# Row norm moved to ScalarE, weight and bias applied on transposed banks: one change to a Trainium2 block kernel

## The chip, the core and the metric

The kernel runs on one core of a Trainium2 chip. The metric is the device time of one execution in microseconds. The engines of the core are TensorE (PE, matmuls and transposes; PEld its weight loads), VectorE (DVE), ScalarE (ACT), GpSimd (POOL) and SyncE (SP, which here only issues DMAs). Each engine runs its own instructions strictly in the order in which they stand in its program, and waits on semaphores for the others.

## The reference, cut to what matters

The input is 1024 rows (two halves H = 0 and 1 of 512 rows, four row blocks of 128 in each) of width 1024. Attention and a depthwise convolution run side by side on a projection of x; their outputs, joined and projected, are added to the scaled residual. The part that the change touches:

```
r  = ALPHA * x + (concat(attention, conv) @ w_out + b_out)
x1 = layer_norm(r) * ln1_g + ln1_b            # over the 1024 columns of a row
u  = x1 @ w_up ; depthwise filter over rows ; silu(gate) * up ; f = (...) @ w_down
r2 = ALPHA * x1 + f                           # then the second layer norm
```

x1 is needed twice: transposed, as the left operand of the up-projection, and in rows, times ALPHA, as the residual of the second norm.

## The kernel before

The work is staged in halves. First come the input projections, convolution and attention of both halves; then `out_proj(0)` and `out_proj(1)` (four column quarters, in each the four row blocks), then the first norm `ln1` of each half, and `up` and `down` of each half. The stages overlap: while `out_proj(0)` runs, attention and the convolution taps of half 1 go on; while `ln1(0)` runs, attention's tail and the convolution's own norm (`conv_norm(1)`, L443 to L472) go on; and `ln1(1)` runs under the up-projection of half 0. A scheduler puts every engine's instructions in an order when the kernel is built, from readiness in its own timeline; nothing is reordered on the chip. So whoever adds an instruction changes the order of its neighbours too.

All matmuls are made in two pieces: a value is rounded to a "high" tensor by a ScalarE cast (`wh`, `oh`, `x`), and the rest, the "low" tensor (`wl`, `ol`), is the difference, taken on GpSimd for weights (L233) and on VectorE for activations (L282). A weight's `wl` therefore stands in GpSimd's queue, and whatever GpSimd does ahead of it delays the matmuls L268 that use it.

What the change touches:

- `out_proj`, L623: the four residual rows of a half are loaded into `acc` and VectorE makes `acc = ALPHA*x + b_out` (128x1024). The products of the two branches are added to `acc` quarter by quarter (L648, L650).
- `ln1`: `row_stats` (L298, L300, and the inverse root on GpSimd, L293), then `layer_norm_rows`: for both halves (LNM 0) VectorE subtracts and scales (L311), GpSimd multiplies by the weight `g1` (L312), VectorE adds the bias (L313). Then `transpose_split`: eight TensorE transposes into two PSUM banks (L278), ScalarE's cast (L281), VectorE's difference (L282). Last ScalarE multiplies the rows by ALPHA (L662).
- Attention's tail on the same engines: softmax sums on VectorE (L510 to L523), the scaling of the probabilities `hank` on GpSimd (L526), their transposes on TensorE (L537), the splits `ph` (L539 ScalarE, L540 VectorE), and the products L558 to L560.
- `up_branch`: products L265, L266 (high weights), L268 (low weights); then the row filter on VectorE (L676, L678) in `z`.
- For half 1 each block's banks are also summed by `other_sums` on VectorE (L747).

Of the kernel before, what the change touches and what calls it, by code (L numbers as in the profile page):

```python
# [15 lines left out]
P = 128  # L16
# [23 lines left out]
KOFF = (4, 5)  # L40
AHEAD = 1
LNM = (0, 0, 1, 1)
XM = (1, 1)
PT = {'x0': 'AT', 'x1': 'AS', 'glu0': 'AS', 'glu1': 'A', 'kv0': 'A', 'kv1': 'A', 'q0': 'A', 'q1': 'A', 'v0': 'T', 'v1': 'T',
      'joint': 'ATSACSYN',
      'tail': 'T', 'out0': 'A', 'out1': 'A', 'ln0': 'A', 'ln1': 'TCN', 'sum1': 'T', 'up0': 'A', 'up1': 'AY', 'down0': 'SY', 'down1': 'S'}
# [23 lines left out]
def hybrid_layer_kernel(  # L70
# [129 lines left out]
    nc.scalar.dma_start(out=pr1[34:78, :], in_=r128(ffn_dw_b))  # L200
    nc.scalar.dma_start(out=pr1[78:122, :], in_=r128(ffn_dw_w[2]))
    nc.scalar.dma_start(out=pr3[0:88, :], in_=ffn_dw_w[0:2].rearrange("k (r c) -> (k r) c", c=P))
    def parameters():
        tp = psB()
        for i, pr in enumerate((pr1, pr2, pr3)):
            nc.tensor.transpose(out=tp[:, i * P:(i + 1) * P], in_=pr, identity=ident)
        nc.vector.tensor_copy(out=par, in_=tp[:, 0:3 * P].rearrange("p (i c) -> p i c", c=P))
        nc.vector.tensor_scalar(out=bq8, in0=par[:, 0, 0:4], scalar1=-0.125, scalar2=None, op0=ALU.mult)

    def pcol(t, i):  # L210
# [9 lines left out]
    fdb = [pcol(0, 34 + i) for i in range(2 * NC)]  # L220
    fw = [[pcol(2, i) for i in range(2 * NC)], [pcol(2, 44 + i) for i in range(2 * NC)],
          [pcol(0, 78 + i) for i in range(2 * NC)]]

    def cdw(k, c):
        return pcol(1, k * 4 + c)
# [45 lines left out]
    def transpose_split(src, xh, xl, t, key):  # L271
        banks = []
        for q in range(2):
            b = psk(key)
            banks.append(b)
            for k in range(4):
                kt = q * 4 + k
                nc.tensor.transpose(out=b[:, k * P:(k + 1) * P], in_=src[:, kt * P:(kt + 1) * P], identity=ident)  # L278
            bv_ = b.rearrange("p (k t) -> p k t", t=P)
            hd = xh[q][:, :, t * P:(t + 1) * P]  # L280
            nc.scalar.copy(out=hd, in_=bv_)  # L281
            nc.vector.tensor_tensor(out=xl[q][:, :, t * P:(t + 1) * P], in0=bv_, in1=f(hd), op=ALU.subtract)  # L282
        return banks
# [370 lines left out]
    def ln1(H, g, b):  # L654
# [2 lines left out]
        x1T[H] = (xh, xl)  # L657
        for t in range(TB):
            a = acc[H * TB + t]
            layer_norm_rows(a, g, b, H)  # L660
            banks = transpose_split(a, xh, xl, t, "ln%d" % H)
            nc.scalar.mul(out=a, in_=a, mul=ALPHA)  # L662
            if H == 1:
                other_sums(t, *[b.rearrange("p (k t) -> p k t", t=P) for b in banks])
            yield
# [316 lines left out]

    def first_norm():
        norm1.extend((bcast_row(ln1_g, 'g1'), bcast_row(ln1_b, 'b1')))
        yield from ln1(0, *norm1)

    def second_conv_norm():
# [86 lines left out]
```

## Time and profile before

| what | value |
| --- | --- |
| median of 3 runs | 1112.66 us (1112.2 to 1114.48) |
| profiled execution | 1113.39 us |
| its span in the trace | 1111.6 us |
| TensorE busy | 1050.4 us, 94% |
| VectorE busy | 788.9 us, 71% |
| ScalarE busy | 481.9 us, 43% |
| GpSimd busy | 654.5 us, 59% |

The profiled execution is 0.7 us above the median, and 1.8 us of it lie outside the span. A matmul's duration is that of a pipelined instruction: rows of one line start closer together than they last. In a timeline a row is start, duration, engine, line, operation, output and inputs, how many, and in brackets the idle time of that engine just before it with what ended it. Durations with x2 or x4 are those of the whole row.

### The profile page before, as it was taken

To read this page: it belongs to the slowest core of one execution; us is meant where nothing else is said; L and a number is where in the kernel's file an instruction comes from. 1 tells how busy PE (TensorE), PEld (TensorE's weight loads), DVE (VectorE), ACT (ScalarE), POOL (GpSimd) and SP (SyncE) were. 2 spreads that over 40 slices of the span, in tenths; PEclk is the share of its full clock that TensorE was granted. 3 is DMA by queue.
4 is the path that set the end of the run, shared out by engine and by line. 5 is a ranking of instruction groups with operands and counts; after the bars stand their busy time and mean duration, and the time that the engine had idled before them with its cause. 6 is when DMAs were issued, how large, how long until landed. Compare 5 with 4: busy or idle time off the path is not lost.

```text
span 1111.6 us, 14383 instructions
## 1 busy us (share of the span) xinstructions
PE 1050.4 (94%) x5113; PEld 873.9 (79%) x5113; DVE 788.9 (71%) x1430; ACT 481.9 (43%) x915; POOL 654.5 (59%) x560
## 2 busy tenths in 40 slices
PE   7999999878968999898999999999999999999996
PEld 5887778778957998676788787878788787888875
DVE  2899789999897448985746656564747566569656
ACT  4546677753548333462515242433425142442430
POOL 3749688775587556455736372746556363636551
PEclk9999999999978999899999999999999999999999
DMA  6535221413600242131211021111212110233321
GB/s 183 160 87 132 77 57 40 139 53 98 186 20 1 78 132 65 50 110 43 76 37 59 20 82 32 58 56 38 76 39 76 35 60 20 76 114 115 113 95 75
DMA packets 115641, 85.19 MB, mean 77 GB/s; under 512 B 20354, under 2 KB 108017, under 8 KB 115569
## 3 DMA queue, kind: packets, MB, share of 16 engines
q1 hardware_dynamic: 112368, 78.92, 23.9%
q10 hardware_dynamic: 3201, 5.35, 1.4%
q8 instruction: 40, 0.66, 0.2%
q14 instruction: 32, 0.26, 0.1%
HBM read 80.05 MB, written 4.21 MB: 76 GB/s over the span
## 4 chain that ended last, share of the span: by engine, by line
PE 76%; DVE 13%; DMA 4%; POOL 3%; ACT 3%; issue 1%; SPq 0%; POOLq 0%; DVEq 0%; ACTq 0%
PE psA L265 6%; PE psA L266 6%; PE psA L268 5%; PE psS L713 2%; PE psS L714 2%; PE psS L715 2%; PE psS L796 2%; PE psS L794 2%; PE psS L793 2%; PE psA L794 2%; PE psA L796 2%; PE psA L793 2%; PE psS L505 2%; PE psA L638 1%; PE psA L713 1%
## 5 line engine op out<-in xcount | busy, mean ns | idle before, releaser
L233 POOL TENSOR_TENSOR wl<-raw,wh 128x512 fp32r<-128x512 f32 x196 | 263.3, 1355 | 162.2 <-ACT wh L231 68.9
L231 ACT CAST wh<-raw 128x512 fp32r<-128x512 f32 x196 | 119.1, 620 | 173.5 <-PE psA L266 24.1
L233 POOL TENSOR_TENSOR wl<-ts,wh 128x512 fp32r<-128x512 f32 x64 | 82.5, 1296 | 155.4 <-ACT wh L231 135.5
L421 DVE SCALAR_TENSOR_TENSOR psC<-hconv,const,psC 128x512 f32<-128x512 f32 x196 | 147.3, 751 | 3.5
L265 PE MATMUL psA<-x,wh 128*128 128x512 f32 x336 | 135.9, 404 | 7.9 <-DVE z L678 4.1
L266 PE MATMUL psA<-x,wh 128*128 128x512 f32 x336 | 134.4, 400 | 0.0
L231 ACT CAST wh<-ts 128x512 fp32r<-128x512 f32 x64 | 39.3, 622 | 177.4 <-PE psS L715 39.2
L268 PE MATMUL psA<-x,wl 128*128 128x512 f32 x336 | 87.2, 396 | 0.6 <-POOL wl L233 0.6
L265 PEld LDWEIGHTS psA<-x,wh 128*128 128x128 f32 x336 | 64.9, 193 | 23.9 <-issue 4.7
L266 PEld LDWEIGHTS psA<-x,wh 128*128 128x128 f32 x336 | 64.9, 193 | 13.5 <-issue 0.2
L268 PEld LDWEIGHTS psA<-x,wl 128*128 128x128 f32 x336 | 62.3, 188 | 15.1 <-issue 1.2
L293 POOL TENSOR_TENSOR tiny<-tiny,const 128x1 f32<-128x1 f32 (+1 forms) x28 | 26.5, 951 | 53.7 <-DVE tiny L292 50.7
L720 DVE TENSOR_TENSOR acc<-psS,acc 128x512 f32<-128x512 f32 x52 | 35.7, 688 | 31.4 <-PE psS L715 31.4
L233 POOL TENSOR_TENSOR ol<-or,oh 128x512 fp32r<-128x512 f32 x32 | 40.7, 1296 | 18.9 <-ACT oh L231 16.6
L793 PE MATMUL psA<-x,wh 128*128 128x512 f32 x112 | 43.6, 389 | 0.0
L794 PE MATMUL psA<-x,wh 128*128 128x512 f32 x112 | 43.6, 389 | 0.0
L793 PE MATMUL psS<-x,wh 128*128 128x512 f32 x112 | 43.6, 389 | 0.0
L794 PE MATMUL psS<-x,wh 128*128 128x512 f32 x112 | 43.6, 389 | 0.0
L832 POOL TENSOR_TENSOR ts<-raw,ts 128x512 f32<-128x512 f32 x32 | 42.0, 1313 | 1.3
L413 POOL TENSOR_TENSOR cp<-cp,cp 128x512 f32<-128x512 f32 x28 | 36.0, 1287 | 8.4 <-ACT cp L409 8.4
L713 PE MATMUL psS<-wh,gh 128*128 128x512 f32 x88 | 35.0, 397 | 5.9 <-ACT gh L693 3.1
L638 PE MATMUL psA<-oh,x 128*128 128x256 f32 x128 | 37.9, 296 | 1.9 <-ACT z L399 1.5
(383 smaller groups left out, 3057.9 us busy)
## 6 DMA issues: line engine op xcount, KB each, us to landing
raw<-in_w_up SPq DMA_DIRECT2D x56, 512.0 KB
raw<-in_w_down SPq DMA_DIRECT2D x28, 512.0 KB
raw<-in_w_in SPq DMA_DIRECT2D x20, 512.0 KB
raw<-in_x SPq DMA_DIRECT2D x8, 512.0 KB
raw<-in_w_in SPq DMA_DIRECT2D x16, 256.0 KB
acc<-in_x SPq DMA_DIRECT2D x8, 512.0 KB
or<-in_w_out SPq DMA_DIRECT2D x64, 64.0 KB
or<-in_w_out SPq DMA_DIRECT2D x8, 512.0 KB
```

The source lines that it names most:

```text
L231: nc.scalar.copy(out=h, in_=part)
L233: nc.gpsimd.tensor_tensor(out=l, in0=part, in1=f(h), op=ALU.subtract)
L265: m.append(nc.tensor.matmul(out=o, lhsT=wh[kt], rhs=xh[kt], start=kt == 0, stop=False))
L266: m.append(nc.tensor.matmul(out=o, lhsT=wh[kt], rhs=xl[kt], start=False, stop=False))
L268: m.append(nc.tensor.matmul(out=o, lhsT=wl[kt], rhs=xh[kt], start=False, stop=kt == KT - 1))
L421: tap(nc.vector.scalar_tensor_tensor(out=dst if k == KO else total, in0=src, scalar=cdw(k, c), in1=total, op0=ALU.mult, op1=ALU.add))
L638: m.append(nc.tensor.matmul(out=pa[:, 0, :], lhsT=yah[:, c, :], rhs=wa[0][c], start=c == 0, stop=False))
L713: m.append(nc.tensor.matmul(out=o, lhsT=gh[:, tsl], rhs=wh, start=j == 0, stop=False))
L793: m.append(nc.tensor.matmul(out=o, lhsT=wh[k], rhs=xh[k], start=k == 0, stop=False))
L794: m.append(nc.tensor.matmul(out=o, lhsT=wh[k], rhs=xl[k], start=False, stop=False))
L796: m.append(nc.tensor.matmul(out=o, lhsT=wl[k], rhs=xh[k], start=False, stop=k == 3))
L832: nc.gpsimd.tensor_tensor(out=t, in0=x0, in1=x1, op=ALU.subtract)
```

## The change

`out_proj` (both halves): ScalarE multiplies the loaded rows by ALPHA, and GpSimd adds the output bias; L623 on VectorE is gone. `ln1` (both halves): VectorE makes only a column, minus mean times inverse deviation (`shift`); ScalarE makes the plain normalised rows with it (one 128x1024 activation in place of L311). The transposes take these rows, and ScalarE multiplies and shifts each 128x128 piece of a transposed bank in place by that piece's weight and bias columns, four per bank, 64 in all, ahead of its cast. The rows that the second residual needs are made behind the transposes, by GpSimd alone: times `g1`, plus `b1`, both of which are scaled by ALPHA once by ScalarE. So L312 of before stays, moved behind the transposes; L313 (VectorE) becomes a GpSimd addition; L662 is gone. Weight and bias also come in as columns, by two more DMAs at the start.

```diff
-XM = (1, 1)
+XM = (0, 0)
...
+    nc.scalar.dma_start(out=pr3[88:96, :], in_=r128(ln1_g))
+    nc.scalar.dma_start(out=pr3[96:104, :], in_=r128(ln1_b))
...
+    l1g = [pcol(2, 88 + i) for i in range(KT)]
+    l1b = [pcol(2, 96 + i) for i in range(KT)]
...
+    def transpose_norm(src, xh, xl, t, key):
+        banks = []
+        for q in range(2):
+            b = psk(key)
+            banks.append(b)
+            for k in range(4):
+                kt = q * 4 + k
+                nc.tensor.transpose(out=b[:, k * P:(k + 1) * P], in_=src[:, kt * P:(kt + 1) * P], identity=ident)
+            for k in range(4):
+                kt = q * 4 + k
+                col = b[:, k * P:(k + 1) * P]
+                nc.scalar.activation(out=col, in_=col, func=AF.Identity, bias=l1b[kt], scale=l1g[kt])
             bv_ = b.rearrange("p (k t) -> p k t", t=P)
             hd = xh[q][:, :, t * P:(t + 1) * P]
             nc.scalar.copy(out=hd, in_=bv_)
...
-            layer_norm_rows(a, g, b, H)
-            banks = transpose_split(a, xh, xl, t, "ln%d" % H)
-            nc.scalar.mul(out=a, in_=a, mul=ALPHA)
+            mv, rstd = row_stats(a)
+            shift = ring("shift1", 1, 2)
+            nc.vector.scalar_tensor_tensor(out=shift, in0=mv[:, 0:1], scalar=-1.0, in1=rstd, op0=ALU.mult, op1=ALU.mult)
+            nc.scalar.activation(out=a, in_=a, func=AF.Identity, bias=shift, scale=rstd)
+            banks = transpose_norm(a, xh, xl, t, "ln%d" % H)
+            nc.gpsimd.tensor_tensor(out=a, in0=a, in1=g, op=ALU.mult)
+            nc.gpsimd.tensor_tensor(out=a, in0=a, in1=b, op=ALU.add)
...
         norm1.extend((bcast_row(ln1_g, 'g1'), bcast_row(ln1_b, 'b1')))
+        for row in norm1:
+            nc.scalar.mul(out=row, in_=row, mul=ALPHA)
```

In the changed kernel the lines stand lower; the new ones are L301 (the activation on a bank), L648 and L649 (residual rows on ScalarE and GpSimd), L685 (`shift`), L686 (rows on ScalarE), L688 and L689 (rows on GpSimd). L549 is the old L526, L424 the old L401, L446 the old L423, L316 the old L293, L238 the old L233, L304 the old L281, L236 the old L231, L297 the old L278, L270 the old L265.

GpSimd at the start of `out_proj(0)`; `vpad` and `x_10` belong to attention, `hank` are its probabilities, `ol` a low weight of `out_proj`. Before:

```order
L381 MEMSET vpad_76_1909 128x512
L293 TENSOR_TENSOR tiny_0_60<-tiny_0_60,const_1_61 128x4
L526 TENSOR_SCALAR hank_34_254<-hank_34_254,tiny_0_60 128x256 x2
L526 TENSOR_SCALAR hank_35_256<-hank_35_256,tiny_0_60 128x256 x2
L401 TENSOR_TENSOR x_10_91<-z_43_342,x_9_90 128x512
L233 TENSOR_TENSOR ol_87_2135<-or_85_2124,oh_86_2133 128x512
```

The same place in the changed kernel:

```order
L649 TENSOR_TENSOR acc_81_2114<-acc_81_2114,bo_80_2112 128x1024
L649 TENSOR_TENSOR acc_82_2118<-acc_82_2118,bo_80_2112 128x1024
L424 TENSOR_TENSOR x_10_93<-z_45_409,x_9_92 128x512
L649 TENSOR_TENSOR acc_83_2122<-acc_83_2122,bo_80_2112 128x1024
L404 MEMSET vpad_76_1911 128x512
L649 TENSOR_TENSOR acc_84_2126<-acc_84_2126,bo_80_2112 128x1024
L316 TENSOR_TENSOR tiny_0_60<-tiny_0_60,const_1_61 128x4
L446 TENSOR_TENSOR cy_73_1511<-cy_73_1511,cp_61_946 128x512
L549 TENSOR_SCALAR hank_34_256<-hank_34_256,tiny_0_60 128x256 x2
L549 TENSOR_SCALAR hank_35_258<-hank_35_258,tiny_0_60 128x256 x2
```

The four bias additions now stand ahead of the probabilities' scaling and of the first low weights.

ScalarE at the end of `ln1(0)`, around the last block's second bank (`psA_3178` before, `psA_3213` after, cast into the part of x1 named `x_38`); `cy`, `x_11` and `nsq` belong to `conv_norm(1)`, `wh` is an up-projection weight. Before:

```order
L281 CAST x_38_262<-psA_3178 128x4x128
L662 ACTIVATE acc_84_2121<-acc_84_2121 128x1024
L539 CAST ph_63_1090<-psT_3227 128x512
L467 ACT_TABLE_LOAD
L467 ACTIVATE cy_72_1508<-cy_72_1508,const_1_61 128x512
```

And in the changed kernel, from that bank's first activation:

```order
L301 ACTIVATE psA_3213<-psA_3213,const_1_61 128x128
L491 ACTIVATE x_11_94<-cy_73_1511,const_1_61 128x512
L495 ACTIVATE nsq_102_2945<-cy_73_1511 128x512
L490 ACTIVATE cy_75_1513<-cy_75_1513,const_1_61 128x512
L236 CAST oh_126_3660<-or_116_3517 128x512
L491 ACTIVATE x_11_94<-cy_74_1512,const_1_61 128x512
L495 ACTIVATE nsq_103_2948<-cy_74_1512 128x512
L301 ACTIVATE psA_3213<-psA_3213,const_1_61 128x128
L491 ACTIVATE x_11_94<-cy_75_1513,const_1_61 128x512
L495 ACTIVATE nsq_104_2951<-cy_75_1513 128x512
L236 CAST wh_25_205<-raw_44_348 128x512
L301 ACTIVATE psA_3213<-psA_3213,const_1_61 128x128 x2
```

Where the cast of the last bank stood ahead of the convolution norm's activations (L467, L468, L472; now L490, L491, L495), it now follows nearly all of them: the bank's cast is the next row. Two units of attention's products, which stood among the matmuls of the first up-projection, now stand ahead of it on TensorE.

GpSimd during `ln1(1)`; `wl_23` is a low weight of the up-projection that runs at the same time. Before:

```order
L312 TENSOR_TENSOR acc_114_3467<-acc_114_3467,g1_105_2972 128x1024
L312 TENSOR_TENSOR acc_115_3470<-acc_115_3470,g1_105_2972 128x1024
L233 TENSOR_TENSOR wl_137_3878<-raw_128_3860,wh_131_3866 128x512
L233 TENSOR_TENSOR wl_146_4384<-raw_133_3870,wh_134_3872 128x512
L233 TENSOR_TENSOR wl_130_3864<-raw_133_3870,wh_136_3876 128x512
L233 TENSOR_TENSOR wl_21_170<-raw_44_346,wh_25_203 128x512
L233 TENSOR_TENSOR wl_23_174<-raw_44_346,wh_27_207 128x512
```

The same place in the changed kernel:

```order
L238 TENSOR_TENSOR wl_21_172<-raw_44_348,wh_25_205 128x512
L688 TENSOR_TENSOR acc_113_3505<-acc_113_3505,g1_105_2978 128x1024
L689 TENSOR_TENSOR acc_113_3505<-acc_113_3505,bo_80_2112 128x1024
L688 TENSOR_TENSOR acc_114_3509<-acc_114_3509,g1_105_2978 128x1024
L238 TENSOR_TENSOR wl_23_176<-raw_44_348,wh_27_209 128x512
L689 TENSOR_TENSOR acc_114_3509<-acc_114_3509,bo_80_2112 128x1024
```

Three row operations stand between two low weights of one product that followed each other before (`b1` shares the buffer named `bo`).

## Rows read from the trace of the kernel before

**Rows 1.** The page's first part: busy time, share and instructions of each engine.
```profile
PE 1050.4 (94%) x5113; PEld 873.9 (79%) x5113; DVE 788.9 (71%) x1430; ACT 481.9 (43%) x915; POOL 654.5 (59%) x560
```

**Rows 2.** Stretches: from:to, length, busy time by engine, granted clock, DMA share, GB/s.
```profile
core 0: us, PE busy (x) PEld busy (x) DVE busy (x) ACT busy (x) POOL busy (x), PEclk, DMA share, GB/s
200.00:300.00 100.00, 88.33 (x635) 80.45 (x634) 93.18 (x215) 52.76 (x141) 66.44 (x77) 0.98 0.35 110
300.00:346.00 46.00, 33.71 (x178) 27.84 (x178) 43.46 (x93) 24.08 (x59) 34.89 (x33) 0.74 0.13 45
346.00:425.00 79.00, 79.00 (x534) 73.12 (x533) 40.94 (x81) 32.34 (x56) 44.43 (x36) 1.00 0.28 84
...
440.00:460.00 20.00, 15.61 (x72) 12.26 (x71) 19.96 (x22) 8.94 (x16) 17.20 (x10) 0.95 0.27 79
```

**Rows 3.** Groups of instructions: busy, mean ns | idle before them, releaser.
```profile
L623 DVE SCALAR_TENSOR_TENSOR acc<-acc,bo 128x1024 f32<-128x1024 f32 x8 | 11.8, 1488 | 1.3 <-DMA acc<-in_x 1.3
L311 DVE TENSOR_SCALAR acc<-acc,tiny 128x1024 f32<-128x1024 f32 x8 | 9.4, 1179 | 1.7 <-POOL tiny L293 1.7
L312 POOL TENSOR_TENSOR acc<-acc,g 128x1024 f32<-128x1024 f32 x8 | 19.8, 2480 | 2.4 <-DVE acc L311 2.4
L313 DVE TENSOR_TENSOR acc<-acc,bo 128x1024 f32<-128x1024 f32 x8 | 14.4, 1798 | 0.6 <-POOL acc L312 0.6
L662 ACT ACTIVATE acc<-acc 128x1024 f32<-128x1024 f32 x8 | 8.6, 1070 | 0.0
L565 ACT ACTIVATE x<-psY,const 128x128 fp32r<-128x128 f32 x32 | 9.1, 366 | 6.2 <-PE psY L560 6.2
```

**Rows 4.** Single lines: minimum/median/maximum duration in ns, first and last start.
```profile
L311 DVE TENSOR_SCALAR acc<-acc,tiny x8: 796/902/1776, 304.6 to 443.0; 128x1024 f32<-128x1024 f32 x8
L313 DVE TENSOR_TENSOR acc<-acc,bo x8: 1195/1410/3361, 312.2 to 454.5; 128x1024 f32<-128x1024 f32 x8
```

**Rows 5.** Timeline of TensorE in `out_proj(0)`: waits for GpSimd and for VectorE.
```profile
225.22 0.38 PE L643 MATMUL psA<-ol,x 128*128 128x256 f32 x1 [0.98 <-POOL ol L233]
...
227.83 0.39 PE L559 MATMUL psY<-ph,vpad 128*128 128x256 f32 x1 [1.19 <-DVE ph L540]
```

**Rows 6.** Timeline of GpSimd around the first half's norm.
```profile
241.25 0.55 POOL L293 TENSOR_TENSOR tiny<-tiny,const 128x1 f32<-128x1 f32 x1 [4.37 <-DVE tiny L292]
...
333.04 4.69 POOL L312 TENSOR_TENSOR acc<-acc,g 128x1024 f32<-128x1024 f32 x2
337.69 2.91 POOL L293 TENSOR_TENSOR tiny<-tiny,const 128x4 f32<-128x4 f32 x2
```

**Rows 7.** Timeline of ScalarE at the end of the first half's norm.
```profile
343.28 1.08 ACT L281 CAST x<-psA 128x512 fp32r<-128x512 f32 x2
...
345.81 1.28 ACT L467 ACT_TABLE_LOAD   x1
347.11 2.23 ACT L467 ACTIVATE cy<-cy,const 128x512 f32<-128x512 f32 x3
349.25 0.71 ACT L468 ACTIVATE x<-cy,const 128x512 fp32r<-128x512 f32 x1
```

**Rows 8.** Timeline of TensorE: attention's last products, first up-projection matmuls.
```profile
345.30 0.28 PE L558 MATMUL psY<-ph,vpad 128*128 128x256 f32 x1
345.42 0.28 PE L559 MATMUL psY<-ph,vpad 128*128 128x256 f32 x1
...
345.66 0.40 PE L265 MATMUL psA<-x,wh 128*128 128x512 f32 x1
345.89 0.40 PE L266 MATMUL psA<-x,wh 128*128 128x512 f32 x1
```

**Rows 9.** Timeline of TensorE during the second half's norm: two waits.
```profile
459.27 0.76 PE L265 MATMUL psA<-x,wh 128*128 128x512 f32 x1 [3.50 <-DVE z L678]
...
474.74 1.19 PE L268 MATMUL psA<-x,wl 128*128 128x512 f32 x4 [0.60 <-POOL wl L233]
```

**Rows 10.** Timeline of ScalarE's queue at the start: a parameter DMA's issue.
```profile
12.09 0.30 ACTq L202 DMA_DIRECT2D early<-in_ffn_dw_w  x1
```

More of the change, by code (lines that the diff above doesn't have):

```diff
@@ L278, in transpose_split @@
                 nc.tensor.transpose(out=b[:, k * P:(k + 1) * P], in_=src[:, kt * P:(kt + 1) * P], identity=ident)
+            bv_ = b.rearrange("p (k t) -> p k t", t=P)
+            hd = xh[q][:, :, t * P:(t + 1) * P]
+            nc.scalar.copy(out=hd, in_=bv_)
+            nc.vector.tensor_tensor(out=xl[q][:, :, t * P:(t + 1) * P], in0=bv_, in1=f(hd), op=ALU.subtract)
+        return banks
+    def transpose_norm(src, xh, xl, t, key):
[10 more added lines that the diff above has]
+                nc.scalar.activation(out=col, in_=col, func=AF.Identity, bias=l1b[kt], scale=l1g[kt])
             bv_ = b.rearrange("p (k t) -> p k t", t=P)
```

## Prediction

> **What bounds the kernel now.** I read the page's first part, then the busy time by stretch, then the groups of the lines that the change touches, and last the timelines of the engines that wait or are waited for there. TensorE is busy for 94% of the span [rows 1], so little can be won over the whole; what can be won lies where TensorE is not full. The stretches show where that is. From 346 to 425 us it is busy for 79.00 of 79.00 us at full clock: nothing there can gain. In `out_proj(0)`, 200 to 300 us (stage A), it stands for 100 - 88.33 = 11.7 us. In the first half's norm, 300 to 346 us (stage B), it stands for 46 - 33.71 = 12.3 us, and the granted clock is 0.74, so that even its busy time is stretched. During the second half's norm, 440 to 460 us (stage C), it stands for 4.4 us at a clock of 0.95 [rows 2]. In all three VectorE is nearly full: 93.18 of 100, 43.46 of 46 and 19.96 of 20 us. ScalarE has 24.08 of 46 in B, GpSimd 34.89 of 46 in B and 17.20 of 20 in C [rows 2]. So the change takes work from the engine that is full there and gives it to two that are not; the question is how full those become, and in what order their queues then stand.
>
> **What leaves VectorE.** L623 is gone, 11.8 us in eight instructions, as are L311 (9.4) and L313 (14.4) [rows 3]: 35.6 us. What is added, eight times a 128x1 column, is priced between zero and the 0.55 us that a 128x1 operation with its start-up takes in GpSimd's row of one [rows 6]; I take little, 1 us in all. Per half that is 5.9 us of L623 and 11.9 us of the norm.
>
> **What comes to GpSimd.** L312 stays (as L688). Two more 128x1024 operations with two inputs per row block, sixteen in all, are of L312's kind and priced at its mean of 2.48 us [rows 3]: 39.7 us, half of it (19.8 us, L649) ahead of or early in the output projections, half (L689) behind the transposes. VectorE's minimum for the like addition is 1.195 us [rows 4]. In the Trainium skill, GPSIMD Engine Reference, section "Engine selection", elementwise work on a tile is put on VectorE, GpSimd being about twice as slow with two inputs: 2480 against 1195 ns here agrees. By that rule alone the two additions would be a loss; it counts engine time, and the stretches of [rows 2] say whose time is scarce.
>
> **What comes to ScalarE.** Eight scalings of residual rows, at L662's 1.07 us [rows 3]; eight row activations of the same size, which replace the eight of L662; 64 activations of 128x128, priced by L565, whose 32 take 9.1 us when they follow each other and 366 ns each when one stands alone [rows 3]: 9.1 to 11.7 us per half. No row shows one that writes into PSUM; below that I see no reason to go far, and I keep 9.1 to 11.7. The two scalings of `g1` and `b1` lie in stage A where ScalarE has 47 us free [rows 2]: no cost there, 2.1 us if that cover were gone. The two parameter DMAs cost about 0.30 us of issuing each [rows 10], between casts; zero to 0.6 us, and I take zero.
>
> **Stage A.** VectorE loses four L623 at the mean of 1.488 us, 6 us [rows 3], of its 93.18 [rows 2]. TensorE's waits there name VectorE (1.19 us for the split `ph`) and GpSimd (0.98 us for a low weight) [rows 5]. The order puts GpSimd's four additions, 4 x 2.48 = 9.9 us, ahead of `hank` and of the low weights of the first quarter: those come later at first. GpSimd has 33.6 us idle in this stretch, and 4.37 us of it in one wait for VectorE [rows 2, 6], so it catches up. The ends are 0 (GpSimd's delay eats the relief) and -8 us (6 us less VectorE work and the waits in its wake); I take **-4**, nearer to VectorE's share.
>
> **Stage B.** Here the price of the new place shows. The gate is the start of the up-projection at 345.66 us, which needs all four row blocks [rows 8]. VectorE is relieved by about 17 us of 43.5. GpSimd is not worse off ahead of the gate: two of its L312 (4.69 us) stood right ahead of four roots that `conv_norm(1)` waits for [rows 6], and most row operations now stand behind them. ScalarE is: 24.1 us busy before; plus four residual rows 4.3; plus 32 bank activations 9.1 to 11.7; four row activations replace four L662 at no net cost. And by the new order the activations of `conv_norm(1)` stand ahead of the last bank's cast, where before that cast ended at 344.4 us and they began after it, at 345.81 [rows 7]. They are a table load of 1.28, four of L467 at 2.23/3 = 0.74, four of L468 at 0.71 and four of L472, of the same shape, at no more than that [rows 7]: 1.3 + 3.0 + 2.8 + 2.8 = 9.9. The sum is 24.1 + 4.3 + 9.1 (11.7) + 9.9 = 47.4 to 50.0 us in a stretch of 46: ScalarE, less than half busy before, is the bound of this stage. Without any gap it ends 1.4 to 4.0 us later than the stage does now; a difference on VectorE follows, 0.6 us (an estimate: half of L313's minimum, which has twice the columns [rows 4]). Two things give time back. The first half of a product needs only the first bank: eight matmuls, spaced 345.89 - 345.66 = 0.23 us, 1.8 us. And twelve matmuls of attention that stood among the up-projection now stand ahead of it, 0.12 us each [rows 8], with two groups of transposes some 2 us, which the full stretch behind no longer holds. So the best end is 1.4 + 0.6 - 1.8 - 2 = -1.8, taken as -2; with gaps in the chain, as it has 22 us of them now [rows 2], it can be +12. I take a start 6 us later less 2 us moved: **+4**.
>
> **Stage C.** VectorE loses about 11.9 - 0.5 = 11 us where it is full. TensorE's greatest wait here, 3.50 us, is for VectorE's row filter [rows 9], and queued ahead of that are the norm's operations. At most the 4.4 us of idle time, the 1 us that a clock of 0.95 takes of 20, and small waits behind come back: -7. Against it, GpSimd has 9.9 us more, and three row operations (7.4 us) and a low weight now stand ahead of `wl_23`, whose matmuls already waited 0.60 us for GpSimd in this kind of place [rows 9]; the product that covers it is 16 matmuls of high weights and four of low ones, 20 x 0.23 = 4.6 us. That would be 7.4 + 1.4 - 4.6 = 4 us late if GpSimd had no lead, none if it has: I take 2. Sum -6 + 2 = **-4**, ends -7 and +3.
>
> **Sum.** -4 + 4 - 4 = -4 us. The profiled execution's 1113.4 becomes 1109.4; it lies 0.7 above the median, so 1112.7 - 4 gives 1108.7, say 1109.
>
> **The rivals.** First, **slower: ScalarE's queue holds the gate.** If the bank activations wait, each for the transposes and for VectorE's part of the convolution norm between them, ScalarE's gaps stay: stage B costs +12, A wins 2 and C 1, +9, so 1122. It decides from the point where the up-projection starts more than 8 us later than its 345.66. For it: the sum above is already over the stretch, and the cast stands last in a queue of waiting work; against it: half the transposes come early, and VectorE, which ScalarE waits for, is freer.
>
> Second, **no difference: VectorE and GpSimd slow each other.** The rows of one kind differ widely: L311 takes 796 to 1776 ns and L313 1195 to 3361 [rows 4], each at one shape. If each of sixteen added operations of GpSimd stretched VectorE's work by half a microsecond, 8 us of the relief are gone, and nearly all of A's and C's gain: 1113. The Trainium skill, GPSIMD Engine Reference, section "Key points", names such contention for VectorE instructions with two SBUF inputs or in a two-port mode. The trace's spread agrees, without proving it; but L311 and L313, the ones stretched most, are themselves removed, which speaks against the rival.
>
> Third, **the whole relief arrives:** B at its -2, A at -8, C at -6: -16, 1097. For it: VectorE's share of 93 to 100% in all three stretches; against: ScalarE's sum in B.
>
> That the change moves work only under TensorE's cover, with no effect, ends at the second rival's time and is counted with it; 79 us of full TensorE behind B speak for it, 28 us of idle time in the three stages against it.
>
> **How the numbers follow.** A run of this kernel can tell about 0.2% (2.2 us) from no change: faster is below 1110.4, slower above 1114.9. Forecast (1104 to 1110): 0.36. Whole relief and near it: 0.14. No difference: 0.20. Slower: 0.30. That makes faster 0.50, same 0.20, slower 0.30. The range leaves out a tenth at each end: 1098 (two thirds of the whole relief's way) to 1121 (the first rival but its last part).
>
> **What would show it.** In the changed profile: VectorE's busy time down by about 34 us, GpSimd's up by about 40, ScalarE's up by 28 to 34. Stage A: TensorE's idle time some 4 us less, GpSimd's waits for VectorE shorter. Stage B: ScalarE over 42 us busy in the 46 ahead of the up-projection's start, that start (relative to the end of stage A) some 6 us later, TensorE's wait there naming ScalarE or the difference after its cast. Stage C: the 3.50 us wait for `z` gone, a wait of some 2 us for a low weight in its place. I am wrong if the up-projection starts earlier than before (ScalarE no bound), or if VectorE's remaining operations beside GpSimd's are longer by half a microsecond each, or if a bank activation takes much other than 0.28 to 0.37 us.

## The result: slower by half a per cent

The changed kernel takes 1117.3 us (median of 20 runs, 1112.98 to 1125.88) against 1112.09 us (20 runs, 1110.45 to 1116.28): ratio 1.005, 95% interval 1.0036 to 1.0064. I had forecast 1109 us, faster. The time lies inside the stated range (1098 to 1121), which was wide enough to hold a loss too, and on the other side of no change: it is the first rival, ScalarE's queue, that came, at somewhat less than its price.

The page of the changed kernel, first part (busy time, share, instructions), answers to [rows 1]:

```profile
PE 1054.6 (94%) x5113; PEld 879.2 (78%) x5113; DVE 774.0 (69%) x1414; ACT 515.5 (46%) x989; POOL 679.7 (61%) x576
```

ScalarE rose by 33.6 us, as foreseen (28 to 34). VectorE fell by 14.9 us where 34 were expected, and GpSimd rose by 25.2 where 40 were: its sixteen added operations took 38.8 us (L649 and L689 below), near their price, and its other operations took less; why is not shown. The profiled execution (span 1120.9, time 1122.71) is 5.4 us above its median, so sizes read from it are those of a long run.

The stretches need care, since the change moves work across a fixed clock time. So I cut both traces at the same instruction: the first product of half 1's output projection (at 371.68 before, 384.48 after), by which time attention, the convolution norm and the first half's norm are done, and the first product of the stage after the second half's norm (498.84 and 506.18). Busy time by stretch, columns as in [rows 2], before:

```profile
300.00:371.68 71.68, 59.39 (x309) 49.63 (x308) 57.44 (x119) 41.50 (x89) 50.65 (x46) 0.83 0.12 37
371.68:498.84 127.16, 121.49 (x717) 106.78 (x715) 96.81 (x163) 49.58 (x84) 71.17 (x52) 0.97 0.29 88
```

and of the changed kernel, with two of the stretches of [rows 2] and the one behind the first wait:

```profile
200.00:300.00 100.00, 91.13 (x638) 83.71 (x636) 95.48 (x215) 61.50 (x151) 81.55 (x84) 0.93 0.39 125
300.00:384.48 84.48, 62.31 (x307) 52.11 (x307) 51.47 (x110) 53.89 (x121) 58.30 (x55) 0.80 0.08 22
350.00:365.00 15.00, 8.49 (x19) 6.04 (x20) 11.40 (x10) 10.60 (x21) 13.67 (x10) 0.50 0.29 80
384.48:506.18 121.70, 118.52 (x714) 104.98 (x713) 85.53 (x154) 62.45 (x116) 73.86 (x52) 1.00 0.29 85
...
440.00:460.00 20.00, 20.00 (x103) 16.86 (x102) 15.58 (x32) 16.88 (x31) 11.89 (x9) 1.00 0.17 53
```

Up to the first cut the changed kernel is 12.8 us late; from there to the second it makes up 127.16 - 121.70 = 5.5 us. The 440 to 460 stretch is TensorE at 20.00 of 20 at full clock, where it stood 4.4 us before: stage C came as forecast. The loss lies ahead of the first cut.

There ScalarE does what the order had shown. Its timeline at the last row block's two banks (four activations and a cast each; L490 is the convolution norm's silu; the rows left out are the convolution norm's, one square of attention and two weight casts):

```profile
346.06 0.97 ACT L301 ACTIVATE psA<-psA,const 128x128 f32<-128x128 f32 x2
...
347.51 0.42 ACT L301 ACTIVATE psA<-psA,const 128x128 f32<-128x128 f32 x1
347.96 1.28 ACT L490 ACT_TABLE_LOAD   x1
...
349.98 0.41 ACT L301 ACTIVATE psA<-psA,const 128x128 f32<-128x128 f32 x1
...
352.15 0.56 ACT L304 CAST x<-psA 128x512 fp32r<-128x512 f32 x1
...
353.33 0.41 ACT L301 ACTIVATE psA<-psA,const 128x128 f32<-128x128 f32 x1
...
357.17 0.42 ACT L301 ACTIVATE psA<-psA,const 128x128 f32<-128x128 f32 x1
...
359.15 0.90 ACT L301 ACTIVATE psA<-psA,const 128x128 f32<-128x128 f32 x2
360.08 0.58 ACT L304 CAST x<-psA 128x512 fp32r<-128x512 f32 x1
```

From the first activation to the end of the second cast, ten instructions of about 0.4 to 0.6 us, it takes 14.6 us (346.06 to 360.66), without an idle moment on ScalarE: nearly all between is the convolution norm, whose result is first used in the output projection of half 1, some 24 us later (TensorE sums its squares at 368.80). TensorE waits for it at each half of the first product:

```profile
352.77 0.80 PE L270 MATMUL psA<-x,wh 128*128 128x512 f32 x1 [6.56 <-ACT x L304]
354.73 0.80 PE L271 MATMUL psA<-x,wh 128*128 128x512 f32 x1 [1.16 <-DVE x L305]
355.32 0.63 PE L270 MATMUL psA<-x,wh 128*128 128x512 f32 x1
355.75 0.63 PE L271 MATMUL psA<-x,wh 128*128 128x512 f32 x1
...
360.72 0.80 PE L270 MATMUL psA<-x,wh 128*128 128x512 f32 x1 [2.41 <-ACT x L304]
```

Behind the waits its matmuls start 0.43 us apart (355.75 - 355.32), where before they started 0.23 us apart [rows 8]: the granted clock was 0.50 from 350 to 365 us, the lower of the two levels, 1.2 GHz, after a stretch in which TensorE mostly waited. The second product begins at 367.21. The first product, 5.6 us long before with one matmul of attention in it, takes 14.4 us.

The groups of the changed lines (busy, mean ns | idle before):

```profile
L301 ACT ACTIVATE psA<-psA,const 128x128 f32<-128x128 f32 x32 | 13.2, 449 | 3.9 <-PE psA L297 3.8
L686 ACT ACTIVATE acc<-acc,tiny 128x1024 f32<-128x1024 f32 x8 | 9.8, 1242 | 2.6 <-DVE tiny L685 2.6
L649 POOL TENSOR_TENSOR acc<-acc,bo 128x1024 f32<-128x1024 f32 x8 | 19.0, 2392 | 0.0
L688 POOL TENSOR_TENSOR acc<-acc,g 128x1024 f32<-128x1024 f32 x8 | 19.1, 2385 | 10.3 <-PE psT L297 5.9 <-PE psA L297 4.5
L689 POOL TENSOR_TENSOR acc<-acc,bo 128x1024 f32<-128x1024 f32 x8 | 19.8, 2470 | 0.2
```

### The profile page after: what moved, and what is told of

The parts are those of the page before. It is cut to its first block, busy times and chain, and to the rows that moved or that the text cites. A ratio compares the mean times of both kernels' runs of the same rounds, so it can differ in the third digit from the quotient of the medians.

```text
span 1120.9 us, 14460 instructions
## 1 busy us (share of the span) xinstructions
PE 1054.6 (94%) x5113; PEld 879.2 (78%) x5113; DVE 774.0 (69%) x1414; ACT 515.5 (46%) x989; POOL 679.7 (61%) x576
## 4 chain that ended last, share of the span: by engine, by line
PE 76%; DVE 9%; ACT 5%; DMA 4%; POOL 4%; issue 1%; SPq 1%; POOLq 0%; ACTq 0%; DVEq 0%
PE psA L270 6%; PE psA L271 6%; PE psA L273 6%; PE psS L740 2%; PE psS L741 2%; PE psS L742 2%; PE psS L823 2%; PE psA L823 2%; PE psA L820 2%; PE psA L821 2%; PE psS L820 2%; PE psS L821 2%; PE psS L528 2%; DMA raw<-in_w_up 1%; PE psA L740 1%
## 5 line engine op out<-in xcount | busy, mean ns | idle before, releaser
L238 POOL TENSOR_TENSOR wl<-raw,wh 128x512 fp32r<-128x512 f32 x196 | 259.4, 1335 | 137.9 <-ACT wh L236 68.8
L236 ACT CAST wh<-raw 128x512 fp32r<-128x512 f32 x196 | 119.1, 620 | 172.4 <-PE psA L271 25.1
L238 POOL TENSOR_TENSOR wl<-ts,wh 128x512 fp32r<-128x512 f32 x64 | 82.5, 1297 | 156.6 <-ACT wh L236 136.8
L270 PE MATMUL psA<-x,wh 128*128 128x512 f32 x336 | 136.3, 406 | 13.3 <-ACT x L304 9.0
L236 ACT CAST wh<-ts 128x512 fp32r<-128x512 f32 x64 | 39.3, 622 | 180.2 <-PE psS L742 39.1
L270 PEld LDWEIGHTS psA<-x,wh 128*128 128x128 f32 x336 | 65.0, 193 | 28.7 <-ACT x L304 9.3
L238 POOL TENSOR_TENSOR ol<-or,oh 128x512 fp32r<-128x512 f32 x32 | 41.1, 1306 | 29.8 <-ACT oh L236 29.7
L316 POOL TENSOR_TENSOR tiny<-tiny,const 128x1 f32<-128x1 f32 (+1 forms) x28 | 22.8, 817 | 47.4 <-DVE tiny L315 47.4
L662 PE MATMUL psA<-ol,x 128*128 128x256 f32 x128 | 37.2, 291 | 2.8 <-POOL ol L238 2.8
```

The lines of the kernel that those rows point to most:

```text
L236: nc.scalar.copy(out=h, in_=part)
L238: nc.gpsimd.tensor_tensor(out=l, in0=part, in1=f(h), op=ALU.subtract)
L270: m.append(nc.tensor.matmul(out=o, lhsT=wh[kt], rhs=xh[kt], start=kt == 0, stop=False))
L662: m.append(nc.tensor.matmul(out=pa[:, 0, :], lhsT=yah[:, c, :], rhs=wa[1][c], start=False, stop=False))
```

## The experiments

Three theories were open. **Q**: the order of ScalarE's queue makes the loss, the last cast behind the convolution norm. **L**: ScalarE's load makes it, whatever the order. **P**: GpSimd's added rows, by holding VectorE or by their own queue.

### The order taken out of the changed kernel

The cast is that of `transpose_norm`, the silu that of `conv_norm`; the edge adds no instruction, it only orders the two on ScalarE. The scheduler also moved a few rows of the same region: on TensorE the sums of the norm's squares and two of attention's stand later among the products.

```diff
-            nc.scalar.copy(out=hd, in_=bv_)
+            last_cast[0] = nc.scalar.copy(out=hd, in_=bv_)
...
-            nc.scalar.activation(out=y[c], in_=y[c], func=AF.Silu, bias=clb[c], scale=clg[c])
+            i = nc.scalar.activation(out=y[c], in_=y[c], func=AF.Silu, bias=clb[c], scale=clg[c])
+            if H == 1:
+                tc.add_manual_dep(i.ins, last_cast[0].ins.name, order, reason="behind the last bank's cast")
```

> The changed kernel with one order edge more: the convolution norm's silu activations of half 1 stand behind the last bank's cast on ScalarE; every other row of the order there stays. Theory Q (the queue order on ScalarE makes the loss: the last bank's activations and cast stand behind the convolution norm's): the up-projection of half 0 starts near 349 us without the second wait of 2.4 us and without the half clock behind it, some 9 us earlier than in the changed kernel's effective start; median 1105 to 1110, ratio to before 0.993 to 0.998. Rival L (ScalarE's load, whatever the order): the 32 activations on the banks cost as much as now, ratio 1.003 or more. Rival P (GpSimd's added rows and VectorE slow each other): no change, ratio about 1.005.

Measured: 1107.05 us, ratio 0.9959 (0.9941 to 0.9978). Q holds, L and P in their full size fall. ScalarE at the same two banks, and the start of the up-projection on TensorE:

```profile
343.36 0.99 ACT L303 ACTIVATE psA<-psA,const 128x128 f32<-128x128 f32 x2
...
346.23 1.83 ACT L303 ACTIVATE psA<-psA,const 128x128 f32<-128x128 f32 x4
...
349.65 0.58 ACT L306 CAST x<-psA 128x512 fp32r<-128x512 f32 x1
350.25 1.28 ACT L492 ACT_TABLE_LOAD   x1
```

```profile
346.39 0.80 PE L270 MATMUL psA<-x,wh 128*128 128x512 f32 x1 [1.66 <-ACT x L306]
```

The two banks now take 6.9 us (343.36 to 350.23) instead of 14.6, a wait of 1.66 us replaces 6.56, and the second wait is gone. The start of 349 us that I expected came at 346.39; the half clock that I expected gone stayed over nearly half of the first product (in starts 0.43 us apart, up to 352.31).

### The order alone, put into the kernel before

Here the cast is that of `transpose_split`, for the last block's second bank; the string changed is the kernel's list of steps, in the order in which they are written, and lets the convolution norm's last step be written ahead of the cast.

```diff
-          'AAAAoAAoNAlAlNAlAlNAAAAfAfAAOOOfsOsssffLLLLffff')
+          'AAAAoAAoNAlAlNAlNAlAAAAfAfAAOOOfsOsssffLLLLffff')
...
-            nc.scalar.copy(out=hd, in_=bv_)
+            cast = nc.scalar.copy(out=hd, in_=bv_)
+            if key == "ln0" and t == 3 and q == 1:
+                tc.add_manual_dep(cast.ins, last_scale[0].ins.name, order, reason="behind the convolution norm")
...
-            nc.scalar.mul(out=yh[c], in_=y[c], mul=gain[4 + c])
+            last_scale[0] = nc.scalar.mul(out=yh[c], in_=y[c], mul=gain[4 + c])
```

> The kernel before, with nothing of the change, but the cast of the last row block's second bank in the first half's norm placed behind the convolution norm's activations on ScalarE, as the changed kernel has it. Theory Q (this place in ScalarE's queue makes the loss by itself): the second half of the first up-projection waits for that cast, some 8 us later than before; the attention products that the order puts into the gap cover up to half: 4 to 9 us slower, ratio 1.003 to 1.008. Rival (the order hurts only together with the added activations): no difference, 0.998 to 1.002.

Measured: 1119.76 us, ratio 1.007 (1.0046 to 1.0094). The order at this place, with nothing of the change, costs as much as the whole change did. ScalarE, and one of TensorE's waits behind it:

```profile
344.89 1.28 ACT L471 ACT_TABLE_LOAD   x1
...
355.03 0.57 ACT L283 CAST x<-psA 128x512 fp32r<-128x512 f32 x1
```

```profile
354.04 0.58 PE L562 MATMUL psY<-ph,vpad 128*128 128x256 f32 x1 [3.77 <-ACT ph L543]
```

The cast of [rows 7] that ended at 344.36 now starts at 355.03. The scheduler moved more than this cast: it put attention products into the gap, ahead of the second half of the first up-projection, and TensorE's waits are for their casts (`ph`), which now stand among the convolution norm's activations in the same queue. So the run shows the price of the norm's place in ScalarE's queue, and not that of the one bank's cast alone.

### Where in the kernel: each half's norm, and the residual rows

The new norm for half 1 only, `NEWH = 1` (half 0 keeps L311 to L313 and L662; `g1` and `b1` scaled behind it):

```diff
+            if H == NEWH:
+                mv, rstd = row_stats(a)
...
+            else:
+                layer_norm_rows(a, g, b, H)
+                banks = transpose_split(a, xh, xl, t, "ln%d" % H)
+                nc.scalar.mul(out=a, in_=a, mul=ALPHA)
```

> The new norm for half 1 only; half 0 has the old one, and the rows g1 and b1 are scaled between the two; residual rows as in the changed kernel. Q and L: the loss of 13 us between the end of the output projection of half 0 and the up-projection goes, the gain of 5 us during the second half's norm stays: ratio 0.992 to 0.997. P: the sixteen residual and bias additions on GpSimd remain but for four, ratio 1.000 to 1.004.

Measured: 1110.47 us, ratio 0.9992 (0.9977 to 1.0007). The loss is gone as Q and L say, but the median shows less of the gain than expected, a miss by 2 to 3 us.

The same with `NEWH = 0`, for half 0 only:

> The new norm for half 0 only; half 1 has the old one (g1 and b1 are scaled back between the two, which changes them by a rounding); residual rows as in the changed kernel. Q and L: all of the loss and none of the gain during the second half's norm: ratio 1.007 to 1.012. P: half of the added GpSimd rows, ratio 1.000 to 1.004.

Measured: 1127.31 us, ratio 1.0134 (1.0107 to 1.0161). All of the loss and none of the gain, a little more than expected.

The new norm for both halves with the residual rows on VectorE (`XM = (1, 1)`):

> The new norm for both halves, but the residual rows stay on VectorE as before. Q and L: the loss lies in the norm of half 0, so it stays, and the relief of VectorE in the output projections goes: ratio 1.004 to 1.010. If the residual rows on ScalarE and GpSimd make the loss instead: ratio 0.995 to 1.001.

Measured: 1113.35 us, ratio 1.0013 (1.0 to 1.0026), a miss: I expected 1.004 at least. The order explains it partly. In this kernel too the silu activations and what follows them stand ahead of casts on ScalarE, but they run earlier, from 337 to 346 us, and the cast that TensorE waits for is one of attention:

```profile
345.24 0.58 PE L581 MATMUL psY<-ph,vpad 128*128 128x256 f32 x1 [6.89 <-ACT ph L562]
```

The up-projection then started at 350.7 us, behind attention's products instead of behind a wait. The same kernel with the silu edge of the first experiment:

> The new norm for both halves, residual rows on VectorE as before, and the convolution norm's silu behind the last bank's cast. Theory Q (queue order on ScalarE): without the edge this kernel was at ratio 1.0013, its TensorE stood 6.9 us waiting for an attention cast that lay behind the convolution norm's activations; with the edge that wait goes, and it gains at least 4 us: ratio 0.993 to 0.9975. Rival R (the residual rows on ScalarE and GpSimd are what the edge only made up for): no gain by the edge here, ratio 1.000 to 1.003.

Measured: 1106.64 us, ratio 0.9948 (0.9929 to 0.9967). Q again: about 0.65% by the edge alone, in a kernel without the row operations. The 6.89 us wait is gone; ahead of the first product TensorE has this left:

```profile
342.97 0.49 PE L271 MATMUL psA<-x,wh 128*128 128x512 f32 x1 [0.22 <-DVE x L307]
```

The new norm for half 1 only, residual rows on VectorE (`XM = (1, 1)`):

> The new norm for half 1 only, residual rows on VectorE as before: only the gain during the second half's norm is left in, with no change at the first half. Q: ratio 0.994 to 0.998. If the relief of VectorE in the output projection of half 0 is worth something of its own, this is slower than the same kernel with the residual rows on ScalarE and GpSimd (0.9992); if those rows cost, it is faster.

Measured: 1107.7 us, ratio 0.9971 (0.9956 to 0.9986). Stage C's gain stands by itself. Against the same kernel with the rows on ScalarE and GpSimd (0.9992) the intervals overlap; a gain by the rows is not seen, rather a cost.

### ScalarE's load, with the order mended

```diff
-            for k in range(4):
-                kt = q * 4 + k
-                col = b[:, k * P:(k + 1) * P]
-                nc.scalar.activation(out=col, in_=col, func=AF.Identity, bias=l1b[kt], scale=l1g[kt])
+            nc.scalar.activation(out=b, in_=b, func=AF.Identity, bias=l1b[q], scale=l1g[q])
```

> The changed kernel with the silu edge, and one activation of 128x512 per bank in place of four of 128x128 (each with one weight and bias column, so x1 is scaled wrongly). Theory L (what is left of the loss ahead of the up-projection is ScalarE's load): 48 activations fewer, about 0.35 us each less about 0.75 us for each whole bank, some 5 us of ScalarE time per half; the up-projection starts 2 to 4 us earlier, ratio 0.990 to 0.994. If only the order counted: 0.995 to 0.997 as with the edge alone.

Measured: 1106.51 us, ratio 0.9951 (0.9932 to 0.9969), above what L asks for and as the edge alone, though the interval reaches into L's range. Half 0's banks took 5.9 us instead of some 13:

```profile
L300 ACT ACTIVATE psA<-psA,const 128x512 f32<-128x512 f32 x8 | 5.9, 760 | 1.5 <-PE psA L299 1.5
```

and the up-projection started 10.8 us earlier than with the edge alone:

```profile
335.56 0.40 PE L270 MATMUL psA<-x,wh 128*128 128x512 f32 x1
```

At the second cut that was 4.6 us (table below), and in the median nothing that can be told. Attention's tail then runs among the up-projection, and TensorE waits 3.70 us for a `ph` there. So the load counts little once the order is right.

### GpSimd's added rows

The bias addition to the rows (L689) left out of the kernel with the silu edge:

> The changed kernel with the silu edge, and the eight GpSimd additions of the bias to the rows left out (the bias is missing in the second residual). Theory P (GpSimd's added rows cost time, by its queue or by slowing VectorE): VectorE's short operations beside it get shorter again and the run gains 2 us or more over the 1107.1 of the kernel with the edge alone. Rival: they lie where they cost nothing, 1106 to 1109.

Measured: 1108.13 us, ratio 0.9959 (0.9942 to 0.9976), the same as with it. P has no price at these eight.

The trace of the changed kernel bears on the other eight. VectorE's addition of 128x4 (the sink to the maxima, softmax), at the end of `out_proj(0)`:

```profile
287.38 6.00 DVE L537 TENSOR_TENSOR tiny<-const,tiny 128x4 f32<-128x4 f32 x1
```

GpSimd over the same time:

```profile
286.71 1.29 POOL L238 TENSOR_TENSOR ol<-or,oh 128x512 fp32r<-128x512 f32 x1
287.97 2.37 POOL L649 TENSOR_TENSOR acc<-acc,bo 128x1024 f32<-128x1024 f32 x1
290.31 0.73 POOL L595 TENSOR_TENSOR sq<-sq 128x256 f32<-128x256 f32 x1
291.00 2.36 POOL L649 TENSOR_TENSOR acc<-acc,bo 128x1024 f32<-128x1024 f32 x1
```

It ends at 293.38, 0.02 us after GpSimd's last: an operation of 0.15 us lasted as long as GpSimd's additions followed each other. TensorE waits for the operation queued behind it:

```profile
294.03 0.39 PE L582 MATMUL psY<-ph,vpad 128*128 128x256 f32 x1 [1.87 <-DVE ph L563]
```

Theory H was that this takes back stage A's gain. First, the residual rows of half 1 on VectorE again (`XM = (0, 1)`), with the silu edge:

> The kernel with the silu edge, and the residual rows of half 1 back on VectorE (those of half 0 stay on ScalarE and GpSimd). Theory H (a VectorE addition of 128x4 with two inputs in SBUF is held while GpSimd's additions for half 1 run back to back: 6.0 us in the changed kernel, against 1.2 at most before, at the end of the output projection of half 0): its longest row falls under 2 us, the 5 us that the output projection had gained by its third quarter are not given back in its last, the up-projection starts 3 to 5 us earlier, median 1102 to 1105. Without H: as the edge alone, 1106 to 1108.

Measured: 1106.46 us, ratio 0.9946 (0.9926 to 0.9966). The longest such row fell from 6.35 us (with the edge alone) to 2.37; the time is the edge's, 0.6 us below it, not 2 to 5. In the profile the up-projection did start 3.4 us earlier than with the edge alone (342.96), as H said, but the last quarter of the output projection had not become shorter (26.5 us, against 19.4), and of the 3.4 us 2.2 are left at the second cut. Then the addition in another form:

```diff
-                nc.vector.tensor_tensor(out=es, in0=sink[:, g * 4:g * 4 + 4], in1=m, op=ALU.add)
+                for j in range(4):
+                    nc.vector.tensor_scalar(out=es[:, j:j + 1], in0=sink[:, g * 4 + j:g * 4 + j + 1],
+                                            scalar1=m[:, j:j + 1], scalar2=None, op0=ALU.add)
```

> The kernel with the silu edge, and the 128x4 addition of the sink to the maxima made as four additions of 128x1, each with one SBUF tensor and a scalar column. Theory H: an operation with one tensor input is not held, each lasts under 0.3 us beside GpSimd's additions, the gain of the output projection is kept: 1102 to 1105. If it is GpSimd's queue and not the VectorE operation that costs: these rows are long too, or the time stays at 1106 to 1108.

Measured: 1114.64 us, ratio 1.0014 (0.9996 to 1.0032), slower than the edge alone. The holding itself is gone, none of 64 rows is long (minimum, median, maximum in ns):

```profile
L542 DVE TENSOR_SCALAR tiny<-const,tiny x64: 198/208/217, 116.8 to 323.7; 128x1 f32<-128x1 f32 x64
```

and the time got worse, so the hold was no loss that this could recover. The edge is in this kernel, and the banks' casts are early; TensorE waits for another operand of the same convolution norm, on VectorE:

```profile
345.95 2.07 PE L486 MATMUL psN<-nz,const 128*128 128x512 f32 x2 [4.79 <-DVE nz L484]
```

> The changed kernel without the silu edge, with the 128x4 addition as four of 128x1 alone. If the held operation and ScalarE's queue order are two separate losses: 3 to 5 us off the changed kernel's 1117.3, 1112 to 1114.5. If the queue order swallows it (the last bank's cast waits for the convolution norm either way): 1116 to 1118.

Measured: 1117.86 us, ratio 1.0043 (1.0025 to 1.0061), as the changed kernel: swallowed, the second of the two answers.

> The new norm for both halves with the silu edge, residual rows on VectorE as before, and the 128x4 addition as four of 128x1. There GpSimd has no additions beside the attention of the output projection, and the longest held row is 1.2 us: H expects no more than 1 us against the 1106.6 of this kernel without it, 1104.5 to 1107.5.

Measured: 1118.74 us, ratio 1.0051 (1.0034 to 1.0069), 12 us slower than without it and far outside what I expected. 48 more instructions made the scheduler put the whole region in another order: the convolution norm's second broadcast, at 333 us without this edit, came at 359 us, and TensorE waited 5.65 us for it:

```profile
359.07 2.08 PE L486 MATMUL psN<-nz,const 128*128 128x512 f32 x2 [5.65 <-DVE nz L484]
```

So these three runs say that the held operation has no price that can be had back in this way; they do not isolate it, since they moved much else. H in its full size falls; what the hold costs stays open. That half a per cent to one hangs on the order in this region is seen once more, and that the silu edge alone does not secure it: with the edge and the split addition the ratios are 1.0014 and 1.0051.

### One table over all runs

Start of the same TensorE instruction in each trace, less that of the kernel before (us): the first product of half 1's output projection (cut 1, 371.68) and the first one after the second half's norm (cut 2, 498.84), the difference of the two, and the measured ratio.

| kernel | cut 1 | cut 2 | between | ratio |
| --- | --- | --- | --- | --- |
| changed kernel | +12.8 | +7.3 | -5.5 | 1.0050 |
| with silu edge | +1.2 | -4.3 | -5.5 | 0.9959 |
| edge, rows on VectorE | -3.8 | -9.2 | -5.4 | 0.9948 |
| edge, rows of half 1 on VectorE | -1.0 | -6.5 | -5.5 | 0.9946 |
| edge, one activation per bank | -5.8 | -8.9 | -3.1 | 0.9951 |
| edge, no row bias | -1.4 | -4.5 | -3.1 | 0.9959 |
| rows on VectorE, no edge | +2.1 | -3.5 | -5.6 | 1.0013 |
| half 0 only | +12.6 | +12.1 | -0.4 | 1.0134 |
| half 1 only | +1.4 | -3.9 | -5.3 | 0.9992 |
| half 1 only, rows on VectorE | -0.4 | -5.7 | -5.3 | 0.9971 |
| edge, addition split | +5.2 | -0.4 | -5.6 | 1.0014 |
| addition split, no edge | +7.6 | +2.1 | -5.5 | 1.0043 |
| edge, rows on VectorE, addition split | +7.5 | +3.5 | -4.0 | 1.0051 |
| before, order alone | +7.8 | +7.5 | -0.3 | 1.0070 |

Between the cuts every kernel with the new norm in half 1 and all its work gains 5.3 to 5.6 us, but for one that gains 4.0, and the two without it half a microsecond at most. Ahead of cut 1 the time goes with the place of the casts, and in the two kernels with both edge and split addition with that of the norm's second broadcast. One profile stands for each kernel, so a cut alone carries the scatter of a run; the ratios carry the verdicts.

## Why the prediction was wrong

**Stage C** was right: -4 forecast, -5.5 measured between the cuts. The 3.50 us wait for `z` of [rows 9] is gone, and a low weight is waited for 0.80 us instead of 0.60, not the 2 us I took:

```profile
481.39 0.98 PE L273 MATMUL psA<-x,wl 128*128 128x512 f32 x3 [0.80 <-POOL wl L238]
```

Without those 2 us the forecast was -6. That it came so near is partly luck: between the cuts TensorE's idle time fell by 2.5 us and its busy time by 3.0, at a granted clock of 1.00 instead of 0.97, where I had set at most 4.4 for the one and 1 for the other.

**Stage A**, -4, did not come: the output projection of half 0 ran from 217.53 to 304.98 us before and from 217.45 to 304.83 in the changed kernel. Inside it there was a gain, and it was lost again. Its first three quarters and its last, before:

```profile
217.53:288.90 71.37, 61.42 (x458) 56.76 (x457) 66.58 (x161) 38.07 (x104) 45.27 (x52) 0.98 0.33 100
288.90:304.98 16.08, 16.08 (x127) 15.27 (x127) 14.93 (x38) 5.53 (x17) 8.38 (x13) 1.00 0.52 176
```

and in the changed kernel:

```profile
217.45:283.51 66.06, 59.53 (x445) 56.35 (x443) 62.96 (x153) 37.84 (x99) 48.87 (x56) 0.92 0.39 112
283.51:304.83 21.32, 19.34 (x138) 17.95 (x137) 19.77 (x46) 11.35 (x30) 18.53 (x21) 0.92 0.35 128
```

The last quarter begins 5.4 us earlier and takes 5.2 us longer. Part of both is order, some twelve instructions of TensorE that stand later; in the last quarter lie also the 6.00 us addition with the 1.87 us wait behind it, and a granted clock of 0.92 instead of 1.00. What each of these took is not shown. The step that failed is "nearer to VectorE's share": of the two ends stated, 0 came. With the silu edge the residual rows on ScalarE and GpSimd give nothing over VectorE (0.9959 against 0.9948, intervals overlap); that stage A's relief is worth anything in the time of the kernel is not shown by any run.

**Stage B**, +4, is the step that failed most, and the whole loss lies in it: stage A ended level, and cut 1 came 12.8 us late in the profile. I had taken a start 6 us later less 2 us moved. The start came 7.1 us later (352.77) and 3.1 us were given back behind the first product, both near what I took. What I put at nothing is that the first product itself grows, from 5.6 to 14.4 us: 7.1 + 8.8 - 3.1 = 12.8. I counted its second bank only as time won ("the first half of a product needs only the first bank"). That bank's cast ended at 360.66, 16.3 us later than the 344.36 of before, and the second half of the product waited for it. Waits inside the product are 1.16 + 2.41 + 0.16 = 3.7 us. Left out altogether was the clock behind the waits: 24 matmuls at mostly 0.43 instead of 0.23 us, up to 24 x 0.2 = 4.8 us, twice the second wait. The stretch in [rows 2] had shown a clock of 0.74 in this stage; I did not price its growing longer.

That the start was near is luck, for the sum that gave it does not hold. I added up ScalarE's busy time (47 to 50 us in 46), called ScalarE the bound and took 6 us of delay from the excess. In the 46 us ahead of the start it was busy for 38.6 us, short of the 42 that I had named as a sign:

```profile
306.77:352.77 46.00, 27.57 (x148) 23.41 (x147) 30.93 (x75) 38.61 (x93) 37.47 (x36) 0.77 0.07 21
```

The four residual rows, 4.3 us of that sum, were not in this stage: all eight had run by 295.5 us. The load was not what counted: the edge that leaves the load as it is and puts the convolution norm behind the cast gives the loss back (1.0050 to 0.9959), and the norm's place in the queue alone, without the load, makes a loss (1.0070). The place had been read from the order, and the right sum follows the casts that TensorE waits for: 14.6 us from the last block's first activation to the end of its last cast, against 6.9 us with the convolution norm out of the way. The rows in [rows 7] gave it: the 9.9 us of table load and twelve activations that I had added to the load stand, all of them, between the two.

**The bank activation** takes 449 ns in the mean, above the 280 to 366 that I took from [rows 3], and the row activation 1242 ns, above 1070; in half 0 the 32 take 13.2 us in place of 9.1 to 11.7. It had little weight: the run with one activation per bank was no faster in the median.

**VectorE's relief** measured 14.9 us. L311, L313 and L623 are gone with their 35.6 us, but rows that stayed grew, by some 19 us in all, over a microsecond for each of GpSimd's sixteen added operations. The 128x4 additions of L537, for one, took 5.9 us before:

```profile
L537 DVE TENSOR_TENSOR tiny<-const,tiny 128x4 f32<-128x4 f32 x16 | 12.1, 758 | 0.0
```

So the second rival's effect is there, larger than the half microsecond per operation at which I set it. No run that took the longest row away became faster, but each of them moved the order too, so what it costs is not shown. The Trainium skill, GPSIMD Engine Reference, section "Key points", names contention for VectorE instructions with two SBUF inputs; the 6.00 us row and the 64 short ones with a single tensor input agree with that.

**The first rival** was right in place and sign: what held the gate was ScalarE's queue, though by the convolution norm's place in it rather than by gaps, for ScalarE had no idle moment at the last two banks. Its +12 for stage B is near the 12.8 of the profile; its sum of +9 is above the +5.2 of the medians, since C won 5.5 instead of 1. Its condition (a start more than 8 us late) was nearly met by the start, 7.1 us late, and passed by the second half of the product, 13.2 us late. I gave it 0.30 and the forecast 0.36. The profiled execution ended 9.3 us later than that of before, where cut 2 came 7.3 us later: the last 2 us or so arise at one wait in the later stages, with low clock behind it; the kernel before waits 1.67 us there:

```profile
686.97 0.79 PE L740 MATMUL psS<-wh,gh 128*128 128x512 f32 x1 [2.44 <-ACT gh L844]
```

What stays open beside the hold: why the residual rows cost 0.4% without the edge (1.0050 against 1.0013) and nothing that can be told with it. The two kernels differ in the order of the whole region.

A version that beats both kernels: the new norm in both halves with the silu edge, residual rows on VectorE (0.9948) or those of half 0 on ScalarE and GpSimd (0.9946), which cannot be told apart.

## What to carry to other kernels

Sum an engine's load to see whether it can be the bound, but price a delay from the queue: take the one instruction that the critical engine waits for, and add up what stands ahead of it from the moment its own input is there. Work that nobody needs soon (here a norm wanted 24 us later) must not stand ahead of it; an edge in the order adds no instruction and can decide the sign of a change, but it secures one place, and the next edit can move the others. After a wait, look at the clock of what follows it as well as at the wait.

## What the hardware showed

- A VectorE addition of 128x4 with two tensors in SBUF, 0.15 us alone, lasted 6.00 us while GpSimd's two-input operations followed each other without a gap, and ended 0.02 us after the last of them. With one tensor and a scalar column, 64 of 64 lasted 198 to 217 ns in kernels with the same GpSimd additions.
- An activation of 128x128 that reads and writes the same PSUM bank took 449 ns in the mean, against 366 ns [rows 3] from PSUM into SBUF in another place of the kernel; one of 128x512 in place took 760 ns. The forms differ also in their scale and bias columns, so what the destination alone costs was not separated: the slower form has one such column more, and an estimate from the row activations below is about 0.1 us for each.
- A row activation of 128x1024 with scale and bias columns took 1242 ns in the mean, against 1049 for a scaling by a constant in the same kernel: 193 ns more for the two columns.
